# All wide products of a block ahead of its narrow ones, and the wide form for the gated feed-forward

## The chip, the core and the metric

One core of one Trainium2 chip runs the whole program. The metric is device time in microseconds. TensorE (PE) does the matrix products, with weight loads (PEld) that overlap them; VectorE (DVE), ScalarE (ACT) and GpSimd (POOL) do the elementwise work, and SyncE (SP) issues the transfers from memory. PSUM is the memory that PE accumulates in, SBUF the on-chip memory that all engines read.

## The reference

Two transformer blocks on 256 tokens of 1024 features, all in fp32. Cut to what the change touches:

```python
def squared_relu_mlp(x, w1, w2):                       # block 1, twice; d_ff = 4096
    return jnp.square(jax.nn.relu(x @ w1)) @ w2
...
# block 1: x = layer_norm(ALPHA*x + mix); ff = squared_relu_mlp(x); pe = sigmoid(x @ gate_w + b) * (p @ proj)
...
# block 2 (one layer)
z = rmsnorm(x) @ w_in                                  # gMLP halves, q, k, v, forget logits, gates
...
merged = gate_a * (a @ w_branch_a) + gate_b * (b @ w_branch_b)
x = x + merged @ w_out
up = rmsnorm(x) @ w_up                                 # 1024 -> 2 * 2816
up = causal_depthwise_conv_2(up, conv_w, conv_b)       # 3 taps along the tokens
act = jax.nn.gelu(up[..., :2816]) * up[..., 2816:]
x = x + act @ w_down
```

## The kernel before

**Split products.** PE multiplies fp32 numbers rounded to a shorter form (`F32R`), so each operand is a pair: `hi`, the rounded number, and `lo`, the rounded remainder. A product is hi·hi + hi·lo + lo·hi. For weights, `unit` loads a block in two halves: a transfer into `raw` (4 buffers), a cast by ACT into `hi` (L141) and a subtraction by DVE into `lo` (L142), in 6 buffers each, which PE frees when it has used them. Activations X lie feature by token, `X.parts(k)` being both parts of 128 features (512 columns) and `X.hi(k)` one (256 columns).

**Two forms of a product with features as output.** A unit is 256 output features in two blocks of 128 (f = 0, 1); each block sums over 8 groups (k) of 128 input features.

- `by_halves` (through `feature_major`) calls `three` (L151 to L153) for each k: three products of 256 columns, 24 a block. Both blocks lie in one PSUM bank, and the code behind them (`evict`) reads PSUM.
- `by_parts` (through `feature_parts`) makes a wide product of 512 columns (L243: weights' `hi` by both parts of X) into both halves of a bank, and a narrow one of 256 columns (L244: weights' `lo` by `X.hi`) into the second half, 8 pairs a block. ACT then copies the first half into `sum` in SBUF (L245), DVE adds the second half to it (L246), and `evict` reads `sum` after both blocks.

Two PSUM banks ("m") serve these outputs in turn; `sum` has two buffers. `by_parts` serves 120 blocks: the first products of both squared-ReLU networks (64), the gMLP half, gates, queries and keys, and the two branches of block 2.

**The two feed-forward networks.** Both run `up(j)` (a first product and its elementwise work) and `down(j)` (24 second products of 512 columns, through `three`, into four banks "a" that stay for the whole network) in the order up 0, then up j+1 and down j, four downs left to the end. In the squared-ReLU network an up is one unit. In the gated one (`conv_ffn`) it is two (q = 0, 1): for each block a scaled copy on ACT (L1029) and two more taps on DVE (L1031) make the convolution, then follow gelu (L1034, ACT), the gating product (L1035, DVE) and the split into `hh` (L1037, ACT) and `hl` (L1038, DVE). It has 11 steps, 44 blocks. In the squared-ReLU network POOL makes `hl` (L451).

The order of each engine's work follows from a scheduler that places the instructions of the code; each engine then runs its own list in order. `ends` holds instructions behind which a few later ones are placed.

Of the kernel before, what the change touches and what calls it, by code (L numbers as in the profile page):

```python
# [10 lines left out]
F32 = mybir.dt.float32  # L11
F32R = mybir.dt.float32r
AF = mybir.ActivationFunctionType
ALU = mybir.AluOpType
AX = mybir.AxisListType
P = 128
T = 256
# [35 lines left out]
def tile_two_blocks(ctx: ExitStack, tc: tile.TileContext, I, tri_d, band_d, sel_d, out):  # L53
    nc = tc.nc
    pe, act, dve, pool, sp = nc.tensor, nc.scalar, nc.vector, nc.gpsimd, nc.sync
# [18 lines left out]
    def work(shape, tag, bufs, dt=F32):  # L74

        return ph[0].tile(shape, dt, tag=tag, bufs=bufs, name=f"{tag}_{next(ids)}")
# [6 lines left out]
    def rows():  # L83
        return kept([P, D], "t")
# [4 lines left out]
    def bank(k):  # L89
        return banks[k].tile([P, 512], F32, tag=k, name=f"ps{k}_{next(ids)}")  # L90
# [4 lines left out]
    def pairs(k):  # L95
        return bank(k).rearrange("p (a t) -> p a t", t=T)
# [18 lines left out]
    def columns(src_rows, n, name):  # L115

        dst = cp.tile([P, n], F32, name=name)
        for i in range(0, n, P):
            c = min(P, n - i)
            src = small([P, P], name="rows")  # L120
            sp.dma_start(src[:c, :], src_rows[i : i + c, :])
            ps = bank("c")
            pe.transpose(ps[:, :c], src[:c, :], ident[:c, :c])
            act.copy(dst[:, i : i + c], ps[:, :c])
        return dst


    def unit(src, a, c, wide=None, behind=()):
        his, los = [], []
        for j in range(2):  # L130
            s = slice(j * a // 2, (j + 1) * a // 2)
            shape = [P, a // 2, c]
            raw = wp.tile(shape, F32, tag="raw", bufs=n_raw, name=f"raw_{next(ids)}")
            if wide:
                hi, lo = work(shape, *wide, F32R), work(shape, *wide, F32R)
            else:
                hi = wp.tile(shape, F32R, tag="hi", bufs=n_w, name=f"hi_{next(ids)}")
                lo = wp.tile(shape, F32R, tag="lo", bufs=n_w, name=f"lo_{next(ids)}")
            sp.dma_start(raw, src[:, s, :])
            with after(*behind):  # L140
                act.copy(hi, raw)  # L141
                dve.tensor_tensor(lo, raw, hi.bitcast(F32), ALU.subtract)  # L142
            his.append(hi)
            los.append(lo)
        return lambda k, cs: (his[2 * k // a][:, k % (a // 2), cs], los[2 * k // a][:, k % (a // 2), cs])

    def rows_of(w, r0, a, c0, c):
        return w[r0 : r0 + a * P, c0 : c0 + c].rearrange("(a p) c -> p a c", p=P)

    def three(o, lh, ll, rh, rl, start, stop):  # L150
        pe.matmul(o, lh, rh, start=start, stop=False)  # L151
        pe.matmul(o, lh, rl, start=False, stop=False)  # L152
        ends["pe"] = pe.matmul(o, ll, rh, start=False, stop=stop).ins  # L153
# [31 lines left out]
    def half(h):  # L185
        return slice(h * P, (h + 1) * P)
# [46 lines left out]
    def by_parts(X, w, c0, evict):  # L233

        w_ = unit(rows_of(w, 0, 8, c0, 256), 8, 256)
        y = work([P, 2, T], "sum", 2)
        for f in range(2):
            ps = pairs("m")  # L240
            for k in range(8):
                wh, wl = w_(k, slice(f * P, (f + 1) * P))
                pe.matmul(ps, wh, X.parts(k), start=k == 0, stop=False)  # L243
                ends["pe"] = pe.matmul(ps[:, 1, :], wl, X.hi(k), start=False, stop=k == 7).ins  # L244
            act.copy(y[:, f, :], ps[:, 0, :])  # L245
            dve.tensor_tensor(y[:, f, :], ps[:, 1, :], y[:, f, :], ALU.add)  # L246
            if f == 1:
                evict(y)
            yield

    def by_halves(X, w, c0, evict, k_bank="m"):

        w_ = unit(rows_of(w, 0, 8, c0, 256), 8, 256)
        ps = pairs(k_bank)
        for f in range(2):
            for k in range(8):
                wh, wl = w_(k, slice(f * P, (f + 1) * P))
                three(ps[:, f, :], wh, wl, X.hi(k), X.lo(k), k == 0, k == 7)
            if f == 1:
                evict(ps)  # L260
            yield

    def feature_major(*args):
        for _ in by_halves(*args):
            pass

    def feature_parts(*args):
        for _ in by_parts(*args):
            pass

    ends = {}
# [144 lines left out]
    def rms_normed(g_ap):  # L416
        g = bcast(g_ap)
        X, xs = Act(), [None, None]

        def tail(h, x):  # L420
            xs[h] = x
            y = kept([P, D], "bc")
            rms_norm(x, g, y)
            X.due[h] = y

        return xs, X, tail
# [586 lines left out]
    def conv_ffn(xs, X, then):  # L1013
        X.flush(1)
        w, wd = I["w_up_2"][0], I["w_down_2"][0]
        taps = columns(I["conv_w_2"][0].rearrange("j (f p) -> (j f) p", p=P), 132, "taps2")
        cb = columns(I["conv_b_2"][0].rearrange("(f p) -> f p", p=P), 44, "cb2")
        ps2 = [[bank("a") for _ in range(2)] for _ in range(2)]
        hts = {}

        def up(j):
            ys = []
            for q in range(2):
                def evict(ps):
                    y = work([P, 2, T], "cy", 4)
                    for f in range(2):
                        ft = 22 * q + 2 * j + f
                        tp = lambda i: taps[:, 44 * i + ft : 44 * i + ft + 1]
                        act.activation(y[:, f, :], ps[:, f, :], AF.Identity, bias=cb[:, ft : ft + 1], scale=tp(2))  # L1029
                        for d in (1, 2):  # L1030
                            dve.scalar_tensor_tensor(y[:, f, d:], ps[:, f, : T - d], tp(2 - d), y[:, f, d:], ALU.mult, ALU.add)  # L1031
                    ys.append(y)
                feature_major(X, w, 2816 * q + 256 * j, evict)
            act.activation(ys[0], ys[0], AF.Gelu_apprx_tanh)  # L1034
            dve.tensor_tensor(ys[0], ys[0], ys[1], ALU.mult)  # L1035
            hh, hl = work([P, 2, T], "hh", 5, F32R), work([P, 2, T], "hl", 5, F32R)
            ends["h_act"] = act.copy(hh, ys[0]).ins  # L1037
            ends["h_dve"] = dve.tensor_tensor(hl, ys[0], hh.bitcast(F32), ALU.subtract).ins  # L1038
            hts[j] = (hh, hl)

        def down(j, w_, h):
            hh, hl = hts[j]
            for k in range(2):
                for c in range(2):
                    rh, rl = w_(k, slice(c * 512, (c + 1) * 512))
                    three(ps2[h][c], hh[:, k, half(h)], hl[:, k, half(h)], rh, rl, j == 0 and k == 0, j == 10 and k == 1)

        n_lag = 4
        up(0)
        for j in range(11 - n_lag):  # L1050
            up(j + 1)
            w_ = unit(rows_of(wd, 256 * j, 2, 0, D), 2, D)
            for h in range(2):
                down(j, w_, h)
        for j in range(11 - n_lag + 1, 11):
            up(j)
        us = [(j, unit(rows_of(wd, 256 * j, 2, 0, D), 2, D, wide=("bw", 8) if j > 8 else None)) for j in range(11 - n_lag, 11)]
        ys = [rows() for _ in range(2)]
        xs1, X1, tail = then()
        for h, js in ((0, us[:3]), (1, us[:1]), (0, us[3:]), (1, us[1:])):  # L1060
            for j, w_ in js:
                if (h, j) == (1, 10):
                    X1.flush(0)
                down(j, w_, h)
            if js[-1][0] < 10:
                continue
            for c in range(2):
                s = slice(c * 512, (c + 1) * 512)
                dve.tensor_tensor(ys[h][:, s], xs[h][:, s], ps2[h][c], ALU.add)
            tail(h, ys[h])  # L1070
        return xs1, X1
# [41 lines left out]
    with phase("pool"):  # L1113
        res = pool_mixer()
        lgs, lbs = I["ln_gain"], I["ln_bias"]
        xs, X, tail = layer_normed(lgs[0, 0], lbs[0, 0])
# [5 lines left out]
    with phase("mlp0"):  # L1122
        xs, X = mlp(0, xs, X, emb, lambda: layer_normed(lgs[0, 1], lbs[0, 1]))
    with phase("gdn"):
        xs, X, emb = gdn(xs, X, lambda: layer_normed(lgs[1, 0], lbs[1, 0]))
    with phase("mlp1"):
        xs, X = mlp(1, xs, X, emb, lambda: layer_normed(lgs[1, 1], lbs[1, 1], I["norm_mix_g_2"][0]))
    with phase("mix"):
        xs, X, emb = mixers(xs, X, lambda: rms_normed(I["norm_ffn_g_2"][0]))
    with phase("ffn"):  # L1130
        xs, X = conv_ffn(xs, X, lambda: rms_normed(I["norm_ple_g_2"][0]))
# [32 lines left out]
```

## Time and profile before

| | |
|---|---|
| median of three runs | 1118.57 us (1118.08 to 1122.54) |
| the profiled execution | 1119.24 us, its span 1117.5 us |
| mean granted clock of PE | 0.997 |
| busy share of PE, DVE, ACT, POOL | 97%, 70%, 55%, 7% |
| products in all | 6578 |

The span is what the profiler saw of the program on the core. A busy share is the time in which at least one instruction of the engine ran; matrix products overlap one another, so the distance between two starts is shorter than a product's duration. L numbers are lines of the kernel.

### The profile page before, as it was taken

To read this page: it belongs to the slowest core of one execution; us is meant where nothing else is said; L and a number is where in the kernel's file an instruction comes from. 1 tells how busy PE (TensorE), PEld (TensorE's weight loads), DVE (VectorE), ACT (ScalarE), POOL (GpSimd) and SP (SyncE) were. 2 spreads that over 40 slices of the span, in tenths; PEclk is the share of its full clock that TensorE was granted. 3 is DMA by queue.
4 is the path that set the end of the run, shared out by engine and by line. 5 is a ranking of instruction groups with operands and counts; after the bars stand their busy time and mean duration, and the time that the engine had idled before them with its cause. 6 is when DMAs were issued, how large, how long until landed. Compare 5 with 4: busy or idle time off the path is not lost. (4 is left out here: it accounts for less than half of the span.)

```text
span 1117.5 us, 17195 instructions
## 1 busy us (share of the span) xinstructions
PE 1088.5 (97%) x6578; PEld 952.1 (85%) x6578; DVE 785.9 (70%) x1253; ACT 609.4 (55%) x1002; POOL 79.3 (7%) x78
## 2 busy tenths in 40 slices
PE   7999999999999999999999999999999999999997
PEld 5688888899998987888888788898888799999986
DVE  5775555678899478655556875587886857777784
ACT  1654444546556554545455556566765655555663
POOL 0001010210201010010112100000000000000000
PEclk9999999999999999999999999999999999999999
DMA  9676656636436137756567556475345645666660
GB/s 338 209 215 187 193 186 192 197 120 184 132 101 196 40 114 237 252 189 191 188 193 230 178 172 189 133 214 163 113 125 178 223 147 181 186 189 181 182 203 38
DMA packets 145249, 197.79 MB, mean 177 GB/s; under 512 B 11135, under 2 KB 117647, under 8 KB 145167
## 3 DMA queue, kind: packets, MB, share of 16 engines
q1 hardware_dynamic: 145167, 196.70, 57.0%
q8 instruction: 51, 0.84, 0.3%
q14 instruction: 31, 0.25, 0.1%
HBM read 195.36 MB, written 1.31 MB: 176 GB/s over the span
## 5 line engine op out<-in xcount | busy, mean ns | idle before, releaser
L142 DVE TENSOR_TENSOR lo<-raw,hi 128x1024 fp32r<-128x1024 f32 (+4 forms) x322 | 383.0, 1198 | 176.6 <-ACT hi L141 172.3
L141 ACT CAST hi<-raw 128x1024 fp32r<-128x1024 f32 (+4 forms) x322 | 330.7, 1031 | 173.9 <-PE psm L243 55.9
L243 PE MATMUL psm<-X,hi 128*128 128x512 f32 x864 | 308.4, 400 | 2.2 <-DVE sum L246 2.2
L244 PE MATMUL psm<-X,lo 128*128 128x256 f32 x864 | 242.2, 280 | 0.0
L243 PEld LDWEIGHTS psm<-X,hi 128*128 128x128 f32 x864 | 162.2, 188 | 44.5 <-DVE sum L246 4.4
L244 PEld LDWEIGHTS psm<-X,lo 128*128 128x128 f32 x864 | 163.1, 189 | 1.1
L153 PE MATMUL psm<-X,lo 128*128 128x256 f32 x448 | 127.1, 284 | 1.0 <-DVE lo L142 1.0
L151 PE MATMUL psm<-X,hi 128*128 128x256 f32 x448 | 126.9, 284 | 0.2 <-ACT X L193 0.2
L152 PE MATMUL psm<-X,hi 128*128 128x256 f32 x448 | 126.9, 283 | 0.0
L151 PE MATMUL psa<-hi,hh 128*128 128x512 f32 x296 | 115.5, 390 | 0.0
L152 PE MATMUL psa<-lo,hh 128*128 128x512 f32 x296 | 115.5, 390 | 0.0
L153 PE MATMUL psa<-hi,hl 128*128 128x512 f32 x296 | 115.2, 389 | 0.0
L153 PEld LDWEIGHTS psm<-X,lo 128*128 128x128 f32 x448 | 85.9, 192 | 1.2 <-DVE lo L142 1.2
L151 PEld LDWEIGHTS psm<-X,hi 128*128 128x128 f32 x448 | 85.8, 192 | 0.8 <-ACT X L193 0.4
L152 PEld LDWEIGHTS psm<-X,hi 128*128 128x128 f32 x448 | 86.0, 192 | 0.3
L152 PE MATMUL psa<-lo,X 128*128 128x512 f32 (+5 forms) x212 | 76.0, 359 | 2.0 <-DVE lo L142 2.0
L245 ACT COPY sum<-psm 128x256 f32<-128x256 f32 x120 | 44.0, 367 | 62.2 <-PE psm L244 61.9
L151 PE MATMUL psa<-hi,X 128*128 128x512 f32 (+5 forms) x212 | 76.2, 360 | 0.7 <-ACT hi L141 0.5
L246 DVE TENSOR_TENSOR sum<-psm,sum 128x256 f32<-128x256 f32 x120 | 50.3, 419 | 37.2 <-ACT sum L245 37.1
L153 PE MATMUL psa<-hi,X 128*128 128x512 f32 (+5 forms) x212 | 76.0, 358 | 0.0
L451 POOL TENSOR_TENSOR hl<-sum,hh 128x512 fp32r<-128x512 f32 x32 | 43.3, 1354 | 331.2 <-ACT hh L450 164.4
L151 PEld LDWEIGHTS psa<-hi,hh 128*128 128x128 f32 x296 | 55.6, 188 | 11.9
(346 smaller groups left out, 1692.3 us busy)
## 6 DMA issues: line engine op xcount, KB each, us to landing
raw<-in_mlp_w_dram SPq DMA_DIRECT2D x128, 512.0 KB, 4.2
raw<-in_w_in_dram SPq DMA_DIRECT2D x48, 512.0 KB, 4.7
raw<-in_w_up_dram SPq DMA_DIRECT2D x44, 512.0 KB, 3.8
raw<-in_gdn_w_in_dram SPq DMA_DIRECT2D x24, 512.0 KB, 4.6
raw<-in_w_down_dram SPq DMA_DIRECT2D x22, 512.0 KB, 4.3
raw<-in_ple_gate_w_dram SPq DMA_DIRECT2D x16, 512.0 KB, 6.3
raw<-in_gdn_w_out_dram SPq DMA_DIRECT2D x8, 512.0 KB, 4.7
raw<-in_w_branch_a_dram SPq DMA_DIRECT2D x8, 512.0 KB, 3.7
```

Of the source, the lines that this page charges most:

```text
L141: act.copy(hi, raw)
L142: dve.tensor_tensor(lo, raw, hi.bitcast(F32), ALU.subtract)
L151: pe.matmul(o, lh, rh, start=start, stop=False)
L152: pe.matmul(o, lh, rl, start=False, stop=False)
L153: ends["pe"] = pe.matmul(o, ll, rh, start=False, stop=stop).ins
L243: pe.matmul(ps, wh, X.parts(k), start=k == 0, stop=False)
L244: ends["pe"] = pe.matmul(ps[:, 1, :], wl, X.hi(k), start=False, stop=k == 7).ins
L245: act.copy(y[:, f, :], ps[:, 0, :])
L246: dve.tensor_tensor(y[:, f, :], ps[:, 1, :], y[:, f, :], ALU.add)
L451: pool.tensor_tensor(hl, r, hh.bitcast(F32), ALU.subtract)
```

## The change

In `by_parts` a block's 8 wide products come first and then its 8 narrow ones. In `conv_ffn` the first product uses `by_parts` instead of `by_halves`, and its convolution reads `sum` in SBUF. POOL makes `hl` of `conv_ffn` instead of DVE. Lines behind the first edit move down by one, so that the narrow product is L245, copy and addition L246 and L247, the taps L1030 and L1032, the split L1038 and L1039.

```diff
         for f in range(2):
             ps = pairs("m")
+            ws = [w_(k, slice(f * P, (f + 1) * P)) for k in range(8)]
             for k in range(8):
-                wh, wl = w_(k, slice(f * P, (f + 1) * P))
-                pe.matmul(ps, wh, X.parts(k), start=k == 0, stop=False)
-                ends["pe"] = pe.matmul(ps[:, 1, :], wl, X.hi(k), start=False, stop=k == 7).ins
+                pe.matmul(ps, ws[k][0], X.parts(k), start=k == 0, stop=False)
+            for k in range(8):
+                ends["pe"] = pe.matmul(ps[:, 1, :], ws[k][1], X.hi(k), start=False, stop=k == 7).ins
             act.copy(y[:, f, :], ps[:, 0, :])
...
-                def evict(ps):
+                def evict(x):
...
-                        act.activation(y[:, f, :], ps[:, f, :], AF.Identity, bias=cb[:, ft : ft + 1], scale=tp(2))
+                        act.activation(y[:, f, :], x[:, f, :], AF.Identity, bias=cb[:, ft : ft + 1], scale=tp(2))
                         for d in (1, 2):
-                            dve.scalar_tensor_tensor(y[:, f, d:], ps[:, f, : T - d], tp(2 - d), y[:, f, d:], ALU.mult, ALU.add)
+                            dve.scalar_tensor_tensor(y[:, f, d:], x[:, f, : T - d], tp(2 - d), y[:, f, d:], ALU.mult, ALU.add)
                     ys.append(y)
-                feature_major(X, w, 2816 * q + 256 * j, evict)
+                feature_parts(X, w, 2816 * q + 256 * j, evict)
...
-            ends["h_dve"] = dve.tensor_tensor(hl, ys[0], hh.bitcast(F32), ALU.subtract).ins
+            ends["h_dve"] = pool.tensor_tensor(hl, ys[0], hh.bitcast(F32), ALU.subtract).ins
```

In the lists of the engines `psm` is a bank of first products, `psa` one of second products, and a number behind a name tells one buffer's use from another; "x4" stands for four alike in a row. PE, first squared-ReLU network, the end of a unit and the begin of the second products behind it, before:

```order
L243 MATMUL psm_524<-X_167,hi_499 128x512
L244 MATMUL psm_524<-X_167,lo_500 128x256
L151 MATMUL psa_432<-hi_549,hh_488 128x512
L152 MATMUL psa_432<-lo_550,hh_488 128x512
L153 MATMUL psa_432<-hi_549,hl_489 128x512
```

The same place of PE after the change, with the whole last block of the unit:

```order
L243 MATMUL psm_524<-X_166,hi_493 128x512 x4
L243 MATMUL psm_524<-X_167,hi_499 128x512 x4
L245 MATMUL psm_524<-X_166,lo_494 128x256 x4
L245 MATMUL psm_524<-X_167,lo_500 128x256 x4
L151 MATMUL psa_432<-hi_549,hh_488 128x512
L152 MATMUL psa_432<-lo_550,hh_488 128x512
```

The wide products moved together to the front of the block; the second products still follow a narrow one. DVE in `conv_ffn`, the elementwise work of one step, before (the two rows with 255 and 254 columns come once for each block):

```order
L142 TENSOR_TENSOR lo_9717<-raw_9715,hi_9716 128x1024
L142 TENSOR_TENSOR lo_9723<-raw_9721,hi_9722 128x1024
L1031 SCALAR_TENSOR_TENSOR cy_9598<-psm_9549,taps_8594,cy_9598 128x255
L1031 SCALAR_TENSOR_TENSOR cy_9598<-psm_9549,taps_8594,cy_9598 128x254
L1031 SCALAR_TENSOR_TENSOR cy_9598<-psm_9549,taps_8594,cy_9598 128x255
L1031 SCALAR_TENSOR_TENSOR cy_9598<-psm_9549,taps_8594,cy_9598 128x254
L1035 TENSOR_TENSOR cy_9530<-cy_9530,cy_9598 128x512
```

And after, from the addition for the first block of a step's first unit (`sum_9855`) to that for the second unit (`sum_9913`):

```order
L247 TENSOR_TENSOR sum_9855<-psm_9856,sum_9855 128x256
L1032 SCALAR_TENSOR_TENSOR cy_9894<-sum_9855,taps_8594,cy_9894 128x255
L1032 SCALAR_TENSOR_TENSOR cy_9894<-sum_9855,taps_8594,cy_9894 128x254
L142 TENSOR_TENSOR lo_10025<-raw_10023,hi_10024 128x1024
L142 TENSOR_TENSOR lo_10031<-raw_10029,hi_10030 128x1024
L247 TENSOR_TENSOR sum_9855<-psm_9875,sum_9855 128x256
L1032 SCALAR_TENSOR_TENSOR cy_9894<-sum_9855,taps_8594,cy_9894 128x255
L247 TENSOR_TENSOR sum_9913<-psm_9914,sum_9913 128x256
```

The additions came in, one for each block, and two subtractions for weights stand between those of the first unit's two blocks.

## The prediction

> **What bounds the kernel now.** I read the page first: the engines' totals, the granted clock, the chain that ended last.
>
> ```profile
> PE 1088.5 (97%) x6578; PEld 952.1 (85%) x6578; DVE 785.9 (70%) x1253; ACT 609.4 (55%) x1002; POOL 79.3 (7%) x78
> PEclk9999999999999999999999999999999999999999
> PE 36%; DMA 2%; DVE 2%; issue 1%; ACT 1%; POOLq 0%; POOL 0%; ACTq 0%; DVEq 0%
> PE psm L243 8%; PE psm L244 4%; PE psm L153 4%; PE psm L152 4%; PE psm L151 4%; PE psa L152 3%; PE psa L153 3%; PE psa L151 3%; DMA raw<-in_w_out_dram 1%; PE psa L952 1%; DVE lo L142 1%; PE psa L927 1%; PE psc L943 0%; DMA raw<-in_w_in_dram
> ...
> L243 PE MATMUL psm<-X,hi 128*128 128x512 f32 x864 | 308.4, 400 | 2.2 <-DVE sum L246 2.2
> L244 PE MATMUL psm<-X,lo 128*128 128x256 f32 x864 | 242.2, 280 | 0.0
> ```
>
> PE is busy 97% of the span at a clock of 0.9 or more in every slice; the chain is nearly all matmuls, and the wide and narrow products wait next to nothing (2.2 and 0.0 us). So time is the number of products times the distance from one start to the next. The mean durations (400, 280 ns) are pipelined and can't be added up, so I took starts from the timeline. First one unit of the first multilayer network between two runs of second products (start, duration, ...):
>
> ```profile
> 120.09 0.39 PE L243 MATMUL psm<-X,hi 128*128 128x512 f32 x1
> 120.32 0.28 PE L244 MATMUL psm<-X,lo 128*128 128x256 f32 x1
> 120.43 0.40 PE L243 MATMUL psm<-X,hi 128*128 128x512 f32 x1
> ...
> 122.90 0.40 PE L243 MATMUL psm<-X,hi 128*128 128x512 f32 x1
> ...
> 125.62 0.28 PE L244 MATMUL psm<-X,lo 128*128 128x256 f32 x1
> 125.73 0.40 PE L151 MATMUL psa<-hi,hh 128*128 128x512 f32 x1
> ...
> 126.89 0.39 PE L153 MATMUL psa<-hi,hl 128*128 128x512 f32 x1
> ...
> 131.20 0.39 PE L243 MATMUL psm<-X,hi 128*128 128x512 f32 x1
> ```
>
> Sixteen pairs go from 120.09 to 125.73: 5.64 us, so 2.82 per 128 features and 352.5 ns a pair. The run of 512-column products after them starts slowly: five intervals from 125.73 to 126.89 take 1.16 us (232 ns each); the next 19, to 131.20, take 4.31 us (226.8 each). So a wide product costs 227 ns once settled, and the switch from narrow to wide about 5 × 5 = 25 ns. Then the gated feed-forward, where every product is 256 columns:
>
> ```profile
> 929.80 0.28 PE L151 MATMUL psm<-X,hi 128*128 128x256 f32 x1
> 939.40 0.28 PE L153 MATMUL psm<-X,lo 128*128 128x256 f32 x1
> 939.52 0.40 PE L151 MATMUL psa<-hi,hh 128*128 128x512 f32 x1
> ...
> 944.99 0.28 PE L151 MATMUL psm<-X,hi 128*128 128x256 f32 x1
> 945.10 0.28 PE L152 MATMUL psm<-X,hi 128*128 128x256 f32 x1
> ```
>
> From 929.80 to 939.40 stand 80 intervals: 9.60 us, 120 ns for a narrow product. The first narrow one behind a wide run took 113 (944.99 to 945.10), as 120.32 to 120.43 did; a few ns saved at that switch.
>
> **The change part by part.** *Order, in the 120 blocks of 128 features that use the split form (the copy's group of 120, below).* Nothing is added or removed; 8 wide and 8 narrow now stand together. After: 8 × 0.227 + 0.025 for the switch + 8 × 0.120 − 0.008 for the other switch = 2.79 us, against 2.82. That is 0.03 × 120 = 3.6 us. The 24 units that follow a run of second products, as at 120.09, don't pay the 25 ns for their first block: 0.6 more. Term one: −4.2 us.
>
> What no row shows is one wide product reading the two-part operand right behind another. Lower bound 227 ns, as the other wide ones; upper bound about 235, an alternating pair less a narrow one of 113 to 120 (232 to 240): at that each block is 8 × 0.235 + 0.95 = 2.83 and the term is +1.2. The wide product at 120.09 reads the two-part operand in a settled run, and the next start came 0.23 later, so I take 227.
>
> A lower bound on the switch is zero: if the 25 ns came from the change of banks and not from the narrow loads, each block would be 2.77 and both terms together some 4 us larger.
>
> *The wide form in the feed-forward.* 44 blocks of 24 narrow products (24 × 0.120 = 2.88 us) become 8 wide and 8 narrow (2.79): −0.09 × 44 = −4.0 us; the seven units behind a run of second products save 0.025 more, −0.2. Term two: −4.1 us. With wide products at 235 it is 0.05 × 44 = 2.2.
>
> Each block adds a copy on ACT and an addition on DVE; the remainder of the hidden vector moves from DVE to POOL. Their rows, and the engines beside PE in the feed-forward (us; PE, PEld, DVE, ACT, POOL busy; clock, DMA share, GB/s):
>
> ```profile
> L245 ACT COPY sum<-psm 128x256 f32<-128x256 f32 x120 | 44.0, 367 | 62.2 <-PE psm L244 61.9
> L246 DVE TENSOR_TENSOR sum<-psm,sum 128x256 f32<-128x256 f32 x120 | 50.3, 419 | 37.2 <-ACT sum L245 37.1
> L451 POOL TENSOR_TENSOR hl<-sum,hh 128x512 fp32r<-128x512 f32 x32 | 43.3, 1354 | 331.2 <-ACT hh L450 164.4
> L1038 DVE TENSOR_TENSOR hl<-cy,hh 128x512 fp32r<-128x512 f32 x11 | 7.5, 684 | 0.7 <-ACT hh L1037 0.7
> 922.00:939.00 17.00, 17.00 (x122) 16.04 (x122) 12.46 (x17) 9.30 (x13) 0.00 (x0) 1.00 0.59 185
> 1031.50:1066.00 34.50, 34.50 (x283) 34.24 (x283) 27.32 (x37) 20.48 (x28) 0.00 (x0) 1.00 0.62 189
> ```
>
> One step j is two units and one run of second products, 17.0 us. DVE gets 4 × 0.42 − 0.68 = +1.0 us: 13.5 of then 16.6 us, 81%. In the stretch of three steps without second products DVE has 27.3 of 34.5; with 3 × 1.0 more and PE at 3 × 4 × 2.79 = 33.5 that is 90%. ACT gets 4 × 0.37 = 1.5 us: 10.8 of 16.6. POOL, idle there, gets 1.35 per step; nothing else is queued behind it, and its result is 0.7 us later but is read by second products a whole step (16 us) later. The convolution on ACT now waits for copy and addition, 0.8 us more, and is a step ahead of its reader too. No transfer is added or moved past another. On average everything stays beside PE at no cost; without that cover it would be 44 × 0.8 us. The cover is thin in two places.
>
> The first: two accumulation banks alternate, and the addition must have read a bank before the block after next begins. In the new order of DVE two remainders of weights (`lo`) stand ahead of the addition that frees the bank of a first unit's second block. The same chain in the network above, where that block began at 122.90:
>
> ```profile
> 125.53 1.23 DVE L142 TENSOR_TENSOR lo<-raw,hi 128x1024 fp32r<-128x1024 f32 x1 [1.54 <-ACT hi L141]
> 126.94 1.23 DVE L142 TENSOR_TENSOR lo<-raw,hi 128x1024 fp32r<-128x1024 f32 x1 [0.19 <-ACT hi L141]
> 128.09 0.42 DVE L246 TENSOR_TENSOR sum<-psm,sum 128x256 f32<-128x256 f32 x1
> ...
> PEld psm L243 <- DVE sum L246: 5.0, 14, 1.6
> ```
>
> The addition ended at 128.51, 5.61 us after its block began; a unit right behind wants the bank after two blocks, 5.64 before and 5.58 after. So it stands on the edge, and over the kernel it cost 5.0 us in 14 waits. In the new order the buffers for `hi` come free after the wide products and ACT is done sooner, but those for `lo` only at the fourth and eighth narrow product, about 2.45 and 2.95 us into the block. Two remainders from 2.5 on (each 1.14 to the next start) and the addition then end about 5.2 to 5.3: 0.3 to spare.
>
> The second: POOL's subtraction and a DVE instruction that reads two operands from SBUF hold each other up.
>
> ```profile
> 213.67 1.22 DVE L142 TENSOR_TENSOR bw<-raw,bw 128x1024 fp32r<-128x1024 f32 x1
> ...
> 214.21 1.84 POOL L451 TENSOR_TENSOR hl<-sum,hh 128x512 fp32r<-128x512 f32 x1 [5.15 <-ACT hh L450]
> ...
> 215.06 2.07 DVE L142 TENSOR_TENSOR bw<-raw,bw 128x1024 fp32r<-128x1024 f32 x1 [0.17 <-ACT bw L141]
> ```
>
> The remainder beside POOL took 2.07 us instead of 1.22. The Trainium skill, "SBUF — State Buffer", section "Who interferes with whom", has this as a lock for a whole instruction between GpSimd's reads and a DVE instruction with two SBUF inputs; the 0.85 us agree, and by that rule the changed convolution steps, which now read `sum` and `cy` from SBUF, fall under it too. One such collision per step, up to 0.85 us, uses up the 0.3 and leaves up to 0.55. If every step met it at the tight place it would cost 0.55 × 11 = 6 us; if none did, nothing. Most of a step's DVE work is not at that place (one of four blocks), so a quarter: +1.5 us.
>
> Sum: −4.2 − 4.1 + 1.5 = −6.8. The transition at the output projection, which waits for transfers, gives back some 0.2 of term one. Against the profiled execution's 1119.24 us (span 1117.5 and 1.7 around it) that is 1112.6 us. That execution lies 0.7 above the median of 1118.57; I don't correct for it.
>
> **Rivals.** *The order is worth nothing* because a wide product on the two-part operand costs 235 in a run too, or because the slow start that follows narrow products swallows it. For it: the first product of the next run always pays (233 and more). Against it: 120.09. Term one 0 to +1.2, term two −2.2, stalls +1.5: 1118.5 to 1119.7. The Trainium skill, "TensorE: Matmul & The Clock Gate", sections "Back-to-back issue gap" and "LDWEIGHTS", goes the same way: N/2.4 + 2.5 ns per product and loads of P/1.2 = 107 ns that hide behind products, hence no price for order; by its figures an estimate of 2.60 instead of 2.62 us per feed-forward block, 0.9 us in all, 1118.3. The trace has 227 and 120 where it has 216 and 109, and 352.5 for a pair instead of 325, so here it is only partly borne out.
>
> *DVE hands half of it back*: the additions queue behind remainders in each step and PE waits 0.4 us in 11 steps (4.4): 1115.5 or, with collisions, up to 1117.
>
> *Slower*: DVE becomes the bound of the feed-forward. Its place is the addition of a unit's second block, behind two remainders, with POOL's lock ahead of them. From 8.3 / 11 = 0.75 us of PE waiting per step the gain is gone; at (8.3 + 5.6) / 11 = 1.26 us it is 0.5% slower, 1124.8. For it: 90% in the stretch without second products. Against it: 81% otherwise, and a collision costs 0.85 less the 0.3 spare.
>
> **Numbers.** 0.5% of the median, 5.6 us, is what a measurement can tell from no change; faster means below 1113.0. Forecast case 0.58 (1110 to 1114; 0.50 of it below 1113.0); a cheap switch, 1107 to 1110, 0.05; order worth nothing 0.20 (1117 to 1119.8, two thirds of it below 1119); half handed back 0.11 (1114 to 1117.5); slower 0.06. Faster 0.55, same 0.39, slower 0.06. The range 1108.5 to 1119 leaves out a little under 0.2: the slower case, a third of the worthless order, part of the cheap switch.
>
> **What will show it.** In the changed trace: wide starts 227 apart in a unit from the sixth on, about 25 ns more over the first five, narrow ones 120; a unit of 5.56 to 5.58 us; a step of the feed-forward of about 16.6 instead of 17.0. PE's wait for the addition stays near 5 us if the forecast holds; 8 or more with the feed-forward's blocks in it means that DVE hands it back. POOL's and DVE's durations in the feed-forward over 1.3 and 1.23 us show collisions. Wide products at 235 throughout would make the forecast wrong from below, a wait of 0.75 us per step from above.

## The result, and the profile after

The changed kernel takes 1107.36 us (median of 4 runs, 1106.14 to 1107.56) against 1118.59 before: ratio 0.9895, 95% interval 0.9875 to 0.9916, 9 to 14 us faster. A repetition gave 1108.08 us against 1118.14, 0.9899 (0.9876 to 0.9922). One run of an experiment below, the feed-forward alone, took 1328.1 us at a granted clock of 0.754 throughout and is left out of its median. The forecast was 1112.6 with 1108.5 as the low end: right in direction, too small, and outside its range.

The page's engines, the chain and the groups that answer to those shown of before:

```profile
PE 1076.8 (97%) x6226; PEld 933.4 (84%) x6226; DVE 791.4 (72%) x1286; ACT 619.1 (56%) x1046; POOL 97.2 (9%) x89
PE 36%; DVE 2%; issue 1%; DMA 1%; ACT 1%; POOL 0%; POOLq 0%; ACTq 0%; DVEq 0%; SPq 0%
L243 PE MATMUL psm<-X,hi 128*128 128x512 f32 x1216 | 305.9, 393 | 2.3 <-DVE sum L247 2.3
L245 PE MATMUL psm<-X,lo 128*128 128x256 f32 x1216 | 170.4, 282 | 0.0
```

PE is the bound as before; 352 products fewer (44 blocks of 24 became 16). PE's wait for the addition is 2.3 us, though four additions a step were added in the gated feed-forward. The idle time of the weight loads for the same reason, 5.0 us in 14 waits before, is 3.7 in 5. The same unit of the first squared-ReLU network as in the prediction, in PE's timeline:

```profile
117.81 1.98 PE L243 MATMUL psm<-X,hi 128*128 128x512 f32 x8
119.62 1.12 PE L245 MATMUL psm<-X,lo 128*128 128x256 f32 x8
120.57 2.00 PE L243 MATMUL psm<-X,hi 128*128 128x512 f32 x8
122.41 1.11 PE L245 MATMUL psm<-X,lo 128*128 128x256 f32 x8
123.36 0.40 PE L151 MATMUL psa<-hi,hh 128*128 128x512 f32 x1
```

Eight wide products behind second products take 1.81 us (226 ns each), behind narrow ones 1.84; eight narrow ones 0.95. So a wide product on the two-part operand costs 227 in a run, the lower bound, and the unit 5.55 us instead of 5.64, as forecast. A step of the gated feed-forward, from the start of one run of second products to the next, before and after:

```profile
956.50 0.40 PE L151 MATMUL psa<-hi,hh 128*128 128x512 f32 x1
```

```profile
930.56 0.40 PE L151 MATMUL psa<-hi,hh 128*128 128x512 f32 x1
...
947.18 0.40 PE L151 MATMUL psa<-hi,hh 128*128 128x512 f32 x1
```

Before, 939.52 (shown in the prediction) to 956.50 is 16.98 us; after, 16.62, forecast 16.6. So far all is as worked out. What was gained besides lies in stages without an edit. Each entry below is the distance between the first products of two stages in the timelines, in us, from two profiles of each kernel (the gated feed-forward counts from the first transpose of its taps, `psc<-ident,rows`, to its last product with `hh`):

| stage | before, again | after, again | difference of means |
|---|---|---|---|
| up to the first wide product | 58.80, 58.02 | 57.09, 57.70 | −1.0 |
| first squared-ReLU network, to the delta net's gate sums | 205.99, 205.98 | 205.02, 205.10 | −0.9 |
| delta net, to the second network's first wide product | 182.67, 184.75 | 179.70, 182.33 | −2.7 |
| second network, to block 2's first transposes | 185.27, 185.07 | 185.74, 185.38 | +0.4 |
| gMLP half, gates, first queries and keys | 134.26, 134.68 | 132.51, 132.66 | −1.9 |
| attention and both branches | 100.06, 100.00 | 99.61, 99.56 | −0.4 |
| output projection, to the feed-forward's first rows | 31.82, 32.03 | 30.99, 30.35 | −1.3 |
| gated feed-forward | 187.81, 187.79 | 184.16, 184.21 | −3.6 |
| the end | 23.30, 23.30 | 23.30, 23.30 | 0 |

The delta net's difference is partly the clock. The windows view of 264 to 272 us (PE, PEld, DVE, ACT, POOL busy; granted clock, DMA share, GB/s) for the kernel before, for the changed one, and for the changed one again:

```profile
264.00:272.00 8.00, 7.21 (x49) 7.24 (x50) 5.88 (x16) 4.61 (x10) 0.00 (x0) 0.79 0.53 175
```

```profile
264.00:272.00 8.00, 8.00 (x71) 8.00 (x70) 7.80 (x12) 5.53 (x12) 0.00 (x0) 1.00 0.23 68
```

```profile
264.00:272.00 8.00, 8.00 (x58) 8.00 (x57) 6.29 (x13) 3.96 (x10) 0.00 (x0) 0.79 0.25 79
```

In two of the three the clock averages 0.79 over 8 us. That is half speed for 3.4 us (shown in the last section), 1.7 us lost. The changed kernel has it in one execution and not in the other, so the edits alone don't decide it. Reading the granted clock in windows of 2 us gives what each execution lost in the delta net: before 1.7 and 3.4 us, after 0 and 1.7. Without it the stage takes 181.0, 181.3 and 179.7, 180.6: −1.0. The stages then sum to −8.7 us, and start and clock add −2.7 in these four profiles.

Two profiles of each kernel are few, and a stage moves by up to 1 us between them. The experiments below gave nine more. Grouped by the order of the products in each stage, with time at half clock taken out, their mean differences from the first network to the feed-forward are −1.1, −0.6, −0.5, −1.5, −0.2, −1.1 and −3.6, in sum −8.6. The sum holds, but in the delta net and in the second network the two groups overlap (delta net 180.4 to 181.3 and 179.7 to 181.0). The record also has the span and the mean granted clock of every run, and their product estimates the time at full clock: 1112.8 us on average in 86 runs of the kernel before, 1103.3 in ten of the changed one, 9.5 less. Span less this product was 4.2 us in the mean before and 2.7 in the changed kernel; about 2 us of it lie behind the last product in all four profiles.

### The profile page after: what moved, and what is told of

Same layout as the page of the kernel before. It is cut to its first block, busy times and chain, and to the rows that moved or that the text cites. A ratio compares the mean times of both kernels' runs of the same rounds, so it can differ in the third digit from the quotient of the medians.

```text
span 1105.8 us, 16550 instructions
## 1 busy us (share of the span) xinstructions
PE 1076.8 (97%) x6226; PEld 933.4 (84%) x6226; DVE 791.4 (72%) x1286; ACT 619.1 (56%) x1046; POOL 97.2 (9%) x89
## 5 line engine op out<-in xcount | busy, mean ns | idle before, releaser
L243 PEld LDWEIGHTS psm<-X,hi 128*128 128x128 f32 x1216 | 220.8, 189 | 45.5 <-DVE sum L247 3.4
L245 PEld LDWEIGHTS psm<-X,lo 128*128 128x128 f32 x1216 | 166.0, 190 | 11.6
L245 PE MATMUL psm<-X,lo 128*128 128x256 f32 x1216 | 170.4, 282 | 0.0
L246 ACT COPY sum<-psm 128x256 f32<-128x256 f32 x164 | 60.0, 366 | 87.2 <-PE psm L245 87.1
L247 DVE TENSOR_TENSOR sum<-psm,sum 128x256 f32<-128x256 f32 x164 | 68.8, 419 | 44.0 <-ACT sum L246 43.5
L153 PEld LDWEIGHTS psa<-hi,hl 128*128 128x128 f32 x296 | 55.6, 188 | 11.8
L152 PEld LDWEIGHTS psa<-lo,hh 128*128 128x128 f32 x296 | 55.7, 188 | 10.3
L451 ACT CAST hh<-sum 128x512 fp32r<-128x512 f32 x32 | 19.9, 622 | 59.5 <-DVE sum L449 59.5
L1032 DVE SCALAR_TENSOR_TENSOR cy<-sum,taps,cy 128x255 f32<-128x255 f32 x88 | 43.6, 506 | 11.4 <-ACT cy L1030 10.7
L152 PEld LDWEIGHTS psa<-lo,X 128*128 128x128 f32 x212 | 39.9, 188 | 7.8 <-DVE lo L142 3.3
L151 PEld LDWEIGHTS psa<-hi,X 128*128 128x128 f32 x212 | 39.8, 188 | 5.9 <-ACT hi L141 1.1
```

The lines of the kernel that those rows point to most:

```text
L243: pe.matmul(ps, ws[k][0], X.parts(k), start=k == 0, stop=False)
L245: ends["pe"] = pe.matmul(ps[:, 1, :], ws[k][1], X.hi(k), start=False, stop=k == 7).ins
L451: act.copy(hh, r)
L1032: dve.scalar_tensor_tensor(y[:, f, d:], x[:, f, : T - d], tp(2 - d), y[:, f, d:], ALU.mult, ALU.add)
```

## The experiments

Theory A: the edited blocks and what they set free earlier gain 8 to 9 us, the rest is where stretches of low clock and the first transfers fall. Theory B: what the stages without an edit gained comes from the change too, with the order of products.

**Each kernel again.** No edit.

> The kernel before, unchanged, profiled a second time. Theory A (the 3 to 4 us that the stages without an edit gained come from where PE's clock gate and the first transfers happen to fall): the second profile shows other stretches at a low granted clock than the first (the first had 0.87 and 0.71 at 264 to 272 us and the double pace of products only from 14.4 us on), and the time stays within 1118 +- 1.5 us. Theory B (they come from the change): the same low stretches at the same places, span 1117.5 +- 0.3.

> The changed kernel, unchanged, profiled a second time. Blocks of first products as before: 5.56 us a unit, 16.61 us a step of the gated feed-forward. Theory A: products reach the double pace at another time than 12.4 us, and a low clock may show at 262 to 270 us; time 1106 to 1110. Theory B: both as in the first profile, time 1107.4 +- 0.3.

Measured 1118.41 us (ratio 1.0002, 0.9983 to 1.0022; profile with a span of 1119.2) and 1108.08 us. The second profile of before had a low stretch more (346 to 351 us), that of the changed kernel one that its first had not: B's fixed pattern falls. Single runs of the kernel before spread from 1115.1 to 1123.9.

**The order alone**: the kernel before with the first edit of the change, the gated feed-forward as it was:

```diff
+            ws = [w_(k, slice(f * P, (f + 1) * P)) for k in range(8)]
             for k in range(8):
-                wh, wl = w_(k, slice(f * P, (f + 1) * P))
-                pe.matmul(ps, wh, X.parts(k), start=k == 0, stop=False)
-                ends["pe"] = pe.matmul(ps[:, 1, :], wl, X.hi(k), start=False, stop=k == 7).ins
+                pe.matmul(ps, ws[k][0], X.parts(k), start=k == 0, stop=False)
+            for k in range(8):
+                ends["pe"] = pe.matmul(ps[:, 1, :], ws[k][1], X.hi(k), start=False, stop=k == 7).ins
```

> Only the order inside the split form; the gated feed-forward as before. Theory A: 120 blocks at 0.03 to 0.045 us less each, 4 to 5.5 us, so 1113 to 1114.5. Theory B: all that the changed kernel gained outside the feed-forward comes with the order, 7 to 8 us: 1110.5 to 1111.5.

1114.04 us, ratio 0.9950 (0.9929 to 0.9970): 4.1 us by the medians, theory A's value, 5.6 by the ratio, whose interval reaches from 3.4 to 7.9 us and so doesn't exclude B's 7 to 8. The time at full clock is 1108.9 us on average, 3.9 below the kernel before, which speaks for A. Its feed-forward took 187.79 us as before, its output projection 30.70.

**The feed-forward alone**, in the split form and with POOL's subtraction, pairs alternating as before in all blocks; its profile is from a run of its own.

> Only the split form in the gated feed-forward, with pairs alternating as before, and POOL's subtraction. 44 blocks at 2.83 instead of 2.88 us: 2.2 us less plus at most 0.5 for blocks behind second products, so 1115.5 to 1116.5 if PE waits for nothing new. If DVE is the bound there, 1118 or more. Both theories give the same here; the waits of PE for the addition tell how near DVE is to the bound.

> The kernel with only the gated feed-forward in the split form, pairs alternating, once more for its profile. The feed-forward from its first row to its last second product took 187.8 us before and 184.2 in the changed kernel. Theory: 44 x (2.88 - 2.826) = 2.4 us less than before, 185.4; of the changed kernel's 3.6 the rest, 1.2 to 1.5, is the order of products. The output projection is as long as before (about 32 us from the projection's first product to the feed-forward), since its blocks alternate.

1115.83 us (median of eleven runs), ratio 0.9975 (0.9960 to 0.9989), 2.3 us, and 2.6 at full clock. In the profile the feed-forward took 186.12 us, 1.7 less than before where 2.4 were expected; the order of its products is then worth 186.12 − 184.2 = 1.9 us. The output projection took 31.83, as in the kernel before. That profiled execution (1121.1 us) lost 6.8 us to half clock in the delta net.

**The last blocks ahead of the output projection alternating**, by a parameter of the split form that says how many wide products stand together:

```diff
-            feature_parts(B, I["w_branch_b_2"][0], 256 * i, ev)
+            feature_parts(B, I["w_branch_b_2"][0], 256 * i, ev, 1)
```

> The changed kernel, with the last eight blocks ahead of the output projection (second branch) alternating as before. Theory: the 1.2 us gained at the output projection, where nothing was edited, come from these blocks: wide products first free the weights' first buffers earlier, so that the casts of the projection's weights start earlier. Then the stretch from the second branch's last unit to the projection's last product is as long as in the kernel before (23 us from the unit's start), 1 to 1.3 us longer than in the changed kernel. Rival, the gain lies in when the transfers land: it stays.

The first product of the output projection and the first rows of the feed-forward behind it, in the timelines of before, of the changed kernel, and of this one:

```profile
867.05 0.48 PE L151 MATMUL psa<-hi,A 128*128 128x512 f32 x1
...
898.87 0.33 PE L123 MATMUL psc<-ident,rows 128*128 128x128 f32 x1 [0.22 <-DVE X L194]
```

```profile
859.66 0.48 PE L151 MATMUL psa<-hi,A 128*128 128x512 f32 x1
...
890.66 0.33 PE L123 MATMUL psc<-ident,rows 128*128 128x128 f32 x1 [0.74 <-DVE X L194]
```

```profile
864.96 0.48 PE L151 MATMUL psa<-hi,A 128*128 128x512 f32 x1
...
897.03 0.33 PE L123 MATMUL psc<-ident,rows 128*128 128x128 f32 x1 [0.87 <-DVE X L194]
```

31.82, 31.00 and 32.07 us. With wide products first ahead of it this stage took 30.35 to 31.38 us in all eight profiles of such kernels, with alternating ones 31.68 to 32.07 in all five. So its gain belongs to the order of the blocks ahead of it. (The one run took 1113.95 us, and its profile lost 5.1 us to half clock, at 41 to 48 and at 266 to 270 us.) What the stage waits for shows in the chain of that stretch, before, after and in this kernel:

```profile
by line: DMA raw<-in_w_out_dram 36.7%; PE psa L152 13.5%; PE psa L153 12.7%; PE psa L151 12.1%; ACT hi L141 5.7%; DVE m L142 4.1%; DVE lo L142 3.6%; DVE G L142 3.6%; ACT m L141 3.1%; issue 3.0%; PE psc L192 2.6%; DVE A L994 2.1%; ACT A L993
```

```profile
by line: DMA raw<-in_w_up_dram 16.6%; PE psa L152 11.9%; DVE lo L142 11.1%; PE psa L153 11.1%; PE psa L151 11.0%; issue 9.6%; PE psm L243 6.4%; ACT hi L141 3.2%; ACT G L141 2.9%; PE psm L245 2.9%; DVE bc L310 2.3%; ACT bc L304 2.2%; DVE t L
```

```profile
by line: DMA raw<-in_w_out_dram 15.7%; PE psa L152 11.9%; PE psa L151 10.4%; PE psa L153 10.4%; DVE G L142 7.1%; DVE m L142 4.2%; DVE lo L142 3.5%; ACT m L141 3.2%; issue 2.7%; PE psc L192 2.6%; DVE A L996 2.1%; DVE sum L248 2.0%; DVE G L99
```

The transfers of its weights carried 37% of the stretch, are not among the larger shares in the changed kernel, and are back with 16% where the last blocks alternate. SP's timelines show when these eight transfers are issued. The seventh, before, after and in this kernel:

```profile
867.59 0.37 SPq L139 DMA_DIRECT2D raw<-in_w_out_dram  x1
```

```profile
858.64 0.37 SPq L139 DMA_DIRECT2D raw<-in_w_out_dram  x1
```

```profile
865.53 0.37 SPq L139 DMA_DIRECT2D raw<-in_w_out_dram  x1
```

Counted from the projection's first product it comes 0.54 us late before, 1.02 us early after, and 0.57 us late here; the fifth and the sixth move by 0.5 and 1.4 us. So the transfers do start earlier. That they do because wide products free the `hi` buffers 0.95 us before a block's end fits, but was not shown by itself.

**Other groupings**: two and two in the first squared-ReLU network (g = 2 below, 8 elsewhere), and in the second, by a form of its own that is not shown, all wide products of both blocks ahead of all narrow ones.

```diff
-            for k in range(8):
-                pe.matmul(ps, ws[k][0], X.parts(k), start=k == 0, stop=False)
-            for k in range(8):
-                ends["pe"] = pe.matmul(ps[:, 1, :], ws[k][1], X.hi(k), start=False, stop=k == 7).ins
+            for k0 in range(0, 8, g):
+                for k in range(k0, k0 + g):
+                    pe.matmul(ps, ws[k][0], X.parts(k), start=k == 0, stop=False)
+                for k in range(k0, k0 + g):
+                    ends["pe"] = pe.matmul(ps[:, 1, :], ws[k][1], X.hi(k), start=False, stop=k == 7).ins
```

> The changed kernel with two other orders in the squared-ReLU networks: in the first network groups of two wide and two narrow products, in the second all 16 wide products of a unit (both blocks) and then its 16 narrow ones. Theory: the price is the switch from narrow to wide, 25 ns spread over the first five wide products (6, 8, 2, 5, 4), less 8 ns at the switch back. Then a unit between second products takes 2 x 2.80 less 0.02 = 5.58 to 5.59 us in the first network and 16 x 0.227 + 16 x 0.120 - 0.008 = 5.54 in the second. Rival 1, the change of the accumulation bank costs the 25 ns: 5.56 to 5.58 in the second. Rival 2, alternation alone is bad and any grouping mends it: 5.56 in the first. In the three units at the end of the second network that follow one another, PE waits for additions in the new order, 0.5 to 2 us in all.

In the second network, PE's timeline (the lines moved):

```profile
471.68 3.79 PE L260 MATMUL psm<-X,hi 128*128 128x512 f32 x16
475.30 2.08 PE L263 MATMUL psm<-X,lo 128*128 128x256 f32 x16
477.22 0.40 PE L151 MATMUL psa<-hi,hh 128*128 128x512 f32 x1
```

5.54 us, the theory's value; rival 1 falls, the change of the bank costs nothing. Groups of two, in the first network:

```profile
85.42 0.63 PE L244 MATMUL psm<-X,hi 128*128 128x512 f32 x2
85.89 0.39 PE L246 MATMUL psm<-X,lo 128*128 128x256 f32 x2
86.11 0.63 PE L244 MATMUL psm<-X,hi 128*128 128x512 f32 x2
86.58 0.40 PE L246 MATMUL psm<-X,lo 128*128 128x256 f32 x2
```

Two wide and two narrow products take 0.69 us (85.42 to 86.11), and the unit 5.56: here rival 2 is right. The first two narrow products behind wide ones come cheap (112 to 119 ns instead of 120), which pays for most of the slower wide ones (231 to 236); only strict alternation costs more, 353 ns a pair against 348 in groups of two. Groups of eight are no better than groups of two. PE waited 2.1 us once and 0.3 us once more for additions in units that follow one another in the second network, more than the 0.02 a unit brings; the one run took 1108.36 us.

**The remainder on DVE again** in the gated feed-forward:

```diff
-            ends["h_dve"] = pool.tensor_tensor(hl, ys[0], hh.bitcast(F32), ALU.subtract).ins
+            ends["h_dve"] = dve.tensor_tensor(hl, ys[0], hh.bitcast(F32), ALU.subtract).ins
```

> The changed kernel with the remainder of the gated feed-forward's hidden vector on DVE again. DVE gets 0.68 us more a step (0.68 of 16.6 us) and loses the collisions with POOL (0.5 us where one was seen). Theory: the addition that frees a bank came 0.1 us before PE wanted it at 927.72, and this remainder is not queued ahead of it in every step: 0 to 2 us slower, 1108 to 1110, PE's wait for the addition below 5 us in the feed-forward. Rival, DVE becomes the bound in the stretch of three steps without second products (90% busy now, 96% then): 1 to 3 us of waits there, 1109 to 1111.

1109.53 us, ratio 0.9923 (0.9901 to 0.9945), not to be told from the changed kernel; its feed-forward took 184.15 us, the same. In the windows view, the step and the stretch of three steps without second products in the changed kernel, and in this one:

```profile
914.00:930.60 16.60, 16.60 (x90) 14.32 (x89) 13.67 (x21) 11.13 (x18) 1.56 (x1) 1.00 0.65 203
1019.10:1052.60 33.50, 33.50 (x194) 29.50 (x193) 30.09 (x46) 23.71 (x40) 5.01 (x3) 1.00 0.63 187
```

```profile
914.40:931.00 16.60, 16.60 (x90) 14.34 (x90) 13.42 (x22) 10.38 (x17) 0.00 (x0) 1.00 0.72 221
1019.60:1053.00 33.40, 33.40 (x194) 29.43 (x193) 29.65 (x49) 23.86 (x40) 0.00 (x0) 1.00 0.62 186
```

DVE is no busier with the subtraction (29.7 of 33.4 us against 30.1 of 33.5): what POOL takes off it, collisions give back. In ten steps DVE spends 6.9 us on these subtractions here; in the changed kernel it spends 7.4 us more than here on the weights' remainders and the taps, of which some run beside POOL. PE waits in neither.

**More work for DVE**: the copy of the first half on DVE, by a parameter of the split form that names the copying instruction, in the gated feed-forward alone.

```diff
-                feature_parts(X, w, 2816 * q + 256 * j, evict)
+                feature_parts(X, w, 2816 * q + 256 * j, evict, dve.tensor_copy)
```

> The changed kernel, with the copy of a block's first half on DVE instead of ACT in the gated feed-forward alone: DVE gets 4 x 0.42 us more a step. By the busy times of the changed kernel that is 15.4 of 16.6 us a step with second products and 35.1 of 33.5 us in the three steps without. Theory (the rival that DVE becomes the bound, now past its point): PE waits for the addition at the place where 0.1 us were to spare, 0.3 to 0.8 us a step, and 1.6 us or more in the last three: the feed-forward takes 4 to 10 us longer, 1111.5 to 1118. If only the average counted: 1.6 us longer, 1109.

1110.29 us, ratio 0.9934 (0.9915 to 0.9952); the feed-forward took 186.28 us, 2.1 longer, near what the average alone gives and short of the theory's 4 to 10. Steps with second products took 16.62 us as in the changed kernel. Most of the loss stands behind them, in the waits of the feed-forward's end:

```profile
PE psc L192 <- DVE bc L310: 1.3, 1, 1.3
```

DVE falls behind in the three steps and comes late to the norm ahead of the next stage. A wait in each step didn't come.

**The split form where DVE is full**: the delta net's convolution, its sums in three buffers that the convolution's output shares.

```diff
-            feature_major(X, w, 256 * i, evict, "ma"[i % 2])
+            feature_parts(X, w, 256 * i, evict, ("cy", 3))
```

> The changed kernel, with the split form also for the 24 blocks of the gated delta net's convolution, where DVE is 95% busy from 300 to 345 us; its copies of the sums share three buffers with the convolution's output. PE saves 24 x 0.09 = 2.2 us of products, DVE gets 24 x 0.42 = 10 us. Theory, the cover is gone there: 3 to 8 us slower than the changed kernel, 1111 to 1116. Rival, DVE's work there is spread so that PE's saving comes through: 1105 to 1106.

1118.25 us, ratio 0.9990 (0.9977 to 1.0004): the whole gain of the change gone, some 10 us slower than the changed kernel and beyond the theory's 3 to 8. The stage took 189.50 us, 7 to 10 more. At full clock the runs lie 4.7 us above the changed kernel's (1108.0 to 1103.3), inside the theory's range; they also lost 5.4 us more to low clock (8.0 to 2.7), which the theory had not counted. From 300 to 345 us, in the changed kernel and in this one:

```profile
300.00:345.00 45.00, 43.07 (x335) 42.02 (x334) 42.73 (x108) 24.06 (x39) 4.25 (x4) 1.00 0.54 159
```

```profile
300.00:345.00 45.00, 38.47 (x212) 32.27 (x211) 42.95 (x105) 25.86 (x46) 0.63 (x1) 1.00 0.45 127
```

DVE was at 95% and stays there; PE falls to 85%. PE's idle time in the stage, 5.3 and 6.1 us in the changed kernel's two profiles, is 12.7 here, and half clock from 379 to 389 us took 5.1 us more.

**The wait ahead of the low clock taken away**, in both kernels: the gate sums, now in a function `gates`, behind the products that followed them.

```diff
+        conv(4), conv(5)
+        with after("pe"):
+            gates()
         for g in range(2):
             for h in range(2):
                 decays(h, g)
         for g in range(2):
-            conv(2 * g + 4), conv(2 * g + 5)
+            if g:
+                conv(6), conv(7)
```

> The changed kernel, with four small products of the gated delta net (gate sums) behind the twelve products that followed them, so that PE works while DVE makes their operand. In the runs so far PE waits 1.2 to 1.8 us for it at 262 to 265 us, and in five of seven profiles without a change there, though not in the same kernel each time, the clock then falls to half for 3 to 4 us, 1.7 us lost. Theory: without the wait no low clock at 262 to 272 us; the delta net takes 178.5 to 180 us from there to the second network instead of 179.7 to 182.3; 1105 to 1107. Rival, the low clock comes at fixed times or from elsewhere: it is seen there again, 1107 to 1108.5.

> The kernel before, with the same move of four small products. If chance in the clock is what the places sum to too little (9 of the 10.5 us between the medians), this kernel loses that wait and that stretch too, and the difference to the changed kernel with the same move is 8.5 to 9.5 us: 1114 to 1116. Rival, the order of products itself keeps the clock up: the low stretches stay here and the difference stays at 10 to 11 us.

1114.14 and 1122.78 us, both slower than without the move (0.9952 and 1.0041 of the kernel before). The low clock at 264 to 272 us is gone in both, as the theory has it (1.00 in the windows there), but PE's waits in the delta net, 5.3 to 7.0 us without the move, are 9.1 and 9.3 in all, and low stretches came at 330 us (kernel before) and at 377 us (changed kernel). The times expected were wrong by 7 to 9 us: I had counted a wait and not the chain of DVE work behind the gate sums. At full clock the move costs 2.0 us in the kernel before and 2.6 in the changed one, and the rest is more time at low clock. The medians differ by 8.6 us, A's 8.5 to 9.5; the ratios differ by 0.0089, 10 us, so this run doesn't tell A from B. The expectation counted the low clock in five of seven profiles; it is in six of the ten taken until then that have the delta net unchanged.

## Why the prediction was right and wrong

**Right: the price of the blocks.** 227 ns for wide, 120 for narrow products, 25 ns at the switch, 5.55 us a unit and 16.62 a step came out as forecast, and the rival that the order is worth nothing fell (order alone: 4 us). What the switch costs was read too simply: by 25 ns at every switch a unit in groups of two would take 5.58 us or more, and it took 5.56. The Trainium skill's spacing in "TensorE: Matmul & The Clock Gate", section "Back-to-back issue gap", depends on the columns alone and so is the same for any order; the runs show 353 against 348 ns a pair, and the measurement decides.

**Wrong: the stall term, +1.5.** It was nothing. The 5.0 us that the prediction read as the cost of the same wait in the kernel before were idle time of the weight loads; PE itself waited 2.4 us there. The tight place is there, as worked out; DVE's timeline, then PE's:

```profile
924.92 2.36 DVE L142 TENSOR_TENSOR lo<-raw,hi 128x1024 fp32r<-128x1024 f32 x2
927.20 0.42 DVE L247 TENSOR_TENSOR sum<-psm,sum 128x256 f32<-128x256 f32 x1
```

```profile
922.14 2.00 PE L243 MATMUL psm<-X,hi 128*128 128x512 f32 x8
...
927.72 0.44 PE L243 MATMUL psm<-X,hi 128*128 128x512 f32 x1
```

The addition ends 5.48 us after its block began and PE takes the bank at 5.58: 0.1 us to spare where I had 0.3. The collisions are there too:

```profile
920.33 1.56 POOL L1039 TENSOR_TENSOR hl<-cy,hh 128x512 fp32r<-128x512 f32 x1 [7.40 <-ACT hh L1038]
```

```profile
921.23 1.73 DVE L142 TENSOR_TENSOR lo<-raw,hi 128x1024 fp32r<-128x1024 f32 x1 [0.50 <-ACT hi L141]
```

The subtraction took 1.73 us instead of 1.22 here and 1.99 in the six steps that follow, but a block earlier than the tight place: POOL's work falls into the first block of the next step. PE waited in no step by more than 0.05 us. Spreading collisions evenly over four blocks was the failing step.

**Wrong: 0.2 given back at the output projection.** It gained 1.3, or 1.1 over all profiles. I took a stage that waits for transfers to be fixed; the issue of its transfers moved with the order of the blocks ahead of it. The delta net gained 1.0 beyond the clock in two profiles of each kernel, 0.6 over all, within what it varies by; its cause wasn't tried.

**Term one was too large in its own stages**: −4.2 forecast, −0.9 + 0.4 − 1.9 − 0.4 = −2.8 found, or −3.3 over all profiles, though each unit saved what it should. Part of that is rounding: 2.82 − 2.793 is 0.027 and not 0.03, which makes 3.2 of the 3.6. Part was lost at the begin of the second network, where two units follow one another and PE waits for an addition. Those two units took 12.31 and 12.74 us in the profiles of the kernel before and 12.75 and 13.47 in those of the changed one; in the other profiles, half clock taken out, they took 12.6 to 12.7 with alternating pairs and 12.2 to 13.4 with wide products first, so how much of it comes with the order stays open. This error made the forecast gain too large, the others made it too small.

**Wrong: the range.** Its low end took in only my prices. By stages the change is worth 8.7 us where I had 6.8; on the execution I started from, that alone gives 1110.5, inside the range. That execution had a low clock and a late start which the changed kernel's first did not have, 1.7 us each, and it lay 0.7 above the median. Of the miss of 5.2 us, 1.9 are then the sum and the rest is such chance; by the runs' time at full clock, 9.5 us, the sum's part is 2.7. The medians differ by 10.1 to 11.2 us, 1.4 to 2.5 more than the stages. Low clock is part of that, 1.5 us less on average in the changed kernel's ten runs. But the kernel with the remainder on DVE, at full clock as fast as the changed one (1103.4 us), lost 5.0 in its six runs, so that low stretches come less often in the changed kernel is not shown.

**The slower rival** didn't come near its point: 0.42 us more a block on DVE cost 2.1 us in all.

## What to carry to other kernels

Take product prices from starts inside runs of one kind and at the switches between kinds; here two wide products in a row are enough to escape the price of alternation, so the order can be chosen by when buffers come free. A form that trades products for vector work pays where the vector engine has room at the right moments (80 to 90% busy was room enough here, 95% was not). When a profile differs in a stage without an edit, look at the clock there and profile the same kernel twice before giving the difference a cause; the product of span and granted clock compares runs that a low clock hit unequally.

## What the hardware showed that I had not expected

In the delta net PE's clock falls to half for 3.4 us at a time, once, twice or not at all in an execution of the same kernel, 1.7 us each. The clock records of the traces also show which execution is hit. The clock becomes full some us into the program, at 14.35 us in the first profile before, and every low stretch of the 13 profiles begins a whole number of 3.413 us later, here at 266.94, which is 74 of them. So time can be laid out in windows of that length, and PE's wait for the gate sums at 262 to 265 us falls into one window or is shared by two. The window with the wait and the next, kernel before; then the two windows that share it in the changed kernel's first profile (columns as above):

```profile
263.52:266.94 3.42, 2.19 (x20) 2.18 (x20) 2.79 (x13) 2.73 (x4) 0.00 (x0) 1.00 0.87 281
266.94:270.35 3.41, 3.41 (x19) 3.41 (x18) 1.92 (x3) 0.47 (x4) 0.00 (x0) 0.50 0.35 103
```

```profile
257.98:261.39 3.41, 2.43 (x21) 2.23 (x19) 3.00 (x11) 1.09 (x2) 0.00 (x0) 1.00 0.80 250
261.39:264.81 3.42, 2.70 (x24) 2.73 (x25) 2.79 (x11) 3.20 (x7) 0.00 (x0) 1.00 0.66 201
```

In the six profiles with half clock here PE was busy for 47% to 64% of the window ahead of it; in the five others that keep the gate sums in place no window here was below 68%. Over all 13 profiles the busy share alone doesn't decide: all seven windows below 50% were followed by half clock, but only 6 of 23 between 50% and 65%, and three stretches began near 378 us behind windows that small products filled to 88% or more. The two states and their length agree with the Trainium skill, "TensorE: Matmul & The Clock Gate", section "What's actually happening", which has a window of 3.4 us that runs freely. That the place of the windows decides which execution is hit fits these profiles; no run here set that place.

Such a stretch is read off a single row: sixteen small products at the same place took 3.52 us in one execution of the changed kernel and 1.95 in a kernel with other orders:

```profile
264.60 3.52 PE L563 MATMUL psc<-tri,gg 128*128 128x128 f32 x16
```

```profile
263.37 1.95 PE L583 MATMUL psc<-tri,gg 128*128 128x128 f32 x16
```

Filling one wait in front of such a stretch removed it there, and others came later: at 330 us behind a window in which PE was busy for 48%, and at 377 us behind one that small products filled.
